# ScalarE's weight casts run one product further ahead of VectorE's low parts, and the first block's transfers go by quarters

## The chip, the core and the metric

The kernel runs on one core of a Trainium2 chip. The metric is device time in microseconds (us) of one execution. The core has five engines with an instruction queue each: TensorE (PE in the profile; its weight loads are PEld), VectorE (DVE), ScalarE (ACT), GpSimd (POOL) and SyncE (SP), which here only issues transfers. Each queue runs in its own order, and engines wait for each other through semaphores. An instruction whose wait is not over holds up all that stands behind it on its engine.

## The reference

One layer of an encoder, on 512 + 256 tokens of width 1024, in float32:

```python
x = layer_norm(ALPHA * x + 0.5 * swiglu(x, ffn1_up, ffn1_down), ln1_g, ln1_b)
u = x @ w_in
...
mix = (jax.nn.sigmoid(gate_a) * h_a + jax.nn.sigmoid(gate_b) * h_b) @ w_out
x = layer_norm(ALPHA * x + mix, ln2_g, ln2_b)
x = layer_norm(ALPHA * x + 0.5 * swiglu(x, ffn2_up, ffn2_down), ln3_g, ln3_b)

def swiglu(x, w_up, w_down):
    gate, up = jnp.split(x @ w_up, 2, axis=-1)
    return (jax.nn.silu(gate) * up) @ w_down
```

The change touches the two feed-forward blocks (`swiglu`, inner width 2816). Between them lie a recurrent branch, a retention branch and their merge, which the diff leaves alone.

## The kernel before, in words

**Numbers in two parts.** A float32 matrix is multiplied as two parts: a high part, which is the value rounded by a cast (`ph` for weights, `xh` or `eh` for inputs), and a low part, which is the value minus the high part (`pl`, `xl`, `el`). ScalarE makes the high part with one copy, VectorE the low part with one subtraction that reads the high part. So a low part always waits for ScalarE. A product is high by high, high by low and low by high: with four pieces of 128 rows it takes 12 matmuls into one bank (`mmt`, L210), eight with `ph` first and four with `pl` last.

**Seven products for eight.** The up projection treats, for each of the 22 column blocks `j`, the gate and the up weights and the two halves of the tokens and of the width as a 2 by 2 by 2 problem, and does it with seven products of 128 x 384 (`pair_items`, numbers 1 to 7). The products 1, 2, 3 and 4 of a `j` take weights as they come, or sums of them; 5, 7, 6 and 3 need sums of weight pieces, which VectorE makes (`combine`, tile `sa`, L376). On the other side, four kinds of input forms (T1, T3, T2, T4, in `forms`) are differences of token halves: for each, VectorE computes a difference (tile `f`, L295), ScalarE casts it (L320) and VectorE makes the low part (L314). They are made once a block, in its first steps, and every later product reads them.

**The order of the work.** `body` puts all products of a block, up and down, in one list of items, and walks over it with a step counter `t`. The queues of ScalarE, VectorE and TensorE are written out in exactly this order. A step does, in turn: the work on the result of product t-1 (`post`: ScalarE copies it to `u` at L414 or applies Silu at L420; VectorE adds at L409), then the transfers that are due (`ahead`, `AHEAD` items ahead), the weight sums that are due (`extra`), both parts of the weights of product t+2 (`prep`), up to three VectorE instructions of the forms (`advance`), and then the matmuls of product t. The first block begins its forms at t = 4 and the second at t = 6 (`FORMS`). The parts `ph` and `pl` have four buffers each, the raw weight pieces (`wr`, 128 x 512, 256 KB) have ten.

**The first items of a block.** For the first six `j` the list opens with twelve products that need no weight sum (`OPEN`: numbers 1 and 2 of each `j`), then 5, 7, 6 of the first two `j`, and then their 3 and 4. The 19th item of the list is product 3 of the first `j`. It adds onto the bank of product 5, which VectorE first has to read: that is the third of three adds after product 6 (L409). All this I call the opening of a block.

**Transfers.** SyncE issues all weight and input transfers in program order. At the very start (`first`, `inputs`) it issues weight pieces of the products 1 and 2 (`wr<-in_f1u`) and the token matrix (`z<-in_xT`, 16 transfers of 128 x 384, 192 KB: eight pieces of the width by two halves of the tokens). A transfer into a `wr` buffer waits until the low part or the sum that last read this buffer is done.

Of the kernel before, what the change touches and what calls it, by code (L numbers as in the profile page):

```python
# [8 lines left out]
F32 = mybir.dt.float32  # L9
F32R = mybir.dt.float32r  # L10
BF16 = mybir.dt.bfloat16
AF = mybir.ActivationFunctionType
ALU = mybir.AluOpType
# [5 lines left out]
P = 128  # L19
D = 1024  # L20
KT = D // P
# [33 lines left out]
TH = T // 2  # L55
LEAD = 6
OPEN = [(1, 0), (1, 1), (1, 2), (1, 3), (2, 0), (2, 1), (1, 4), (1, 5), (2, 2), (2, 3), (2, 4), (2, 5)]
FORMS = {True: 4, False: 6}
RAWS = 10
AHEAD = 9  # L60
GATED = 6
KEEPO = 4
TQ = 2
# [8 lines left out]
class Builder:  # L72
# [44 lines left out]
    def load(self, name, shape, pool=None):  # L117
        t = (pool or self.const).tile(shape, F32, name=self.nm(name))
        self.nc.sync.dma_start(t, self.I[name])
        return t  # L120
# [209 lines left out]
    def ffn(self, ctx, z, xs, idx, up, down, after, start, own, then=None):  # L330
        nc = self.nc
        chunks, j = [], 0
# [5 lines left out]
        m = KT // 2  # L338
        xe, fw = self.pool(ctx, "xe", 1), self.pool(ctx, "fw", 1)
# [25 lines left out]
                raws[j, part, h], = raw(up[j, :, part, h * m:h * m + m])  # L365
            return raws[j, part, h]

        def pieces(src):
            n = src.shape[-1]
            h, l = (fw.tile([P, m * P], F32R, tag=t, name=self.nm(t), bufs=4)[:, :n] for t in ("ph", "pl"))  # L370
            self.split(src, h, l)
            return tuple(t.rearrange("p (a b) -> p a b", b=P) for t in (h, l))

        def combine(a, b, op, out=None):
# [4 lines left out]
        def pair_items(j):  # L379
            early = j < LEAD  # L380
            st = {}

            def sum_of(n):
                def run():
                    g0, g1, u0, u1 = [load(j, p, h) for p in range(2) for h in range(2)]
                    if n == 1:
                        st[1] = combine(u0, u1, ALU.add)
                    elif n == 3:
                        st[3] = combine(g0, u0, ALU.subtract)
                    elif n == 2:  # L390
                        st[2] = combine(st[1], g0, ALU.subtract, st[1] if early else None)
                    else:
                        st[4] = combine(g1, st[2], ALU.subtract, st[2] if early else None)
                return run
# [5 lines left out]
            def bank_of(n):  # L400
                key = {1: "A", 2: "A", 5: "C", 3: "C", 7: "D", 4: "D", 6: "B"}[n]
                if key not in st:
# [3 lines left out]
            src = {1: lambda: load(j, 0, 0), 2: lambda: load(j, 0, 1), 4: lambda: load(j, 1, 1),  # L406
                   5: lambda: st[1], 7: lambda: st[3], 6: lambda: st[2], 3: lambda: st[4]}
# [32 lines left out]
            items = {}  # L440
            of = {5: 1, 7: 3, 6: 2, 3: 4}
            for n in (1, 5, 7, 6, 2, 3, 4):
                def mm(w, n=n):
                    alloc()
                    ps = bank_of(n)
                    self.mmt(ps, self.terms(w, X[xof[n]]), ((0, TH),), n not in (2, 3, 4), True, n in (2, 3, 4))
                    if early and n < 3:
                        raws.pop((j, 0, n - 1))
                need = (sum_of(of[n]), 3 if early else 6 + (n in (6, 3))) if n in of else None
                get = (lambda n=n: load(j, 0, n - 1)) if early and n < 3 else None  # L450
                items[n] = src[n], mm, *(lambda n=n, f=f: f(n) for f in (post, late, after_late)), need, get, xof[n]
            return items, lambda: [load(j, p, h) for p in range(2) for h in range(2)]
# [32 lines left out]
        def body():  # L485
# [16 lines left out]
            for i, it in enumerate(items):  # L502
                if it[6]:
                    fetch.setdefault(i, []).append(it[6])
                if it[5]:
                    extra.setdefault(max(i - it[5][1], -2), []).append(it[5][0])
            steps = self.forms(z, xs, ext, hp, own)

            def advance(t):
# [21 lines left out]
                        f()  # L531

            def prep(t):
                if t < len(items):
                    ready[t] = pieces(items[t][0]())

            ahead(0)
            with self.tc.manual_schedule(engines={E.Activation, E.DVE, E.PE}):
                for t in range(-2, len(items) + 1):
                    if t > 0:  # L540
                        items[t - 1][2]()
                    for f in afters:
                        f()
                    ahead(t)
                    if then and t == 100:
                        with self.tc.issue_after(self.mark):
                            then()
                    for f in extra.get(t, ()):
                        f()
                    prep(t + 2)  # L550
                    advance(t)
                    if t > 0:
                        items[t - 1][3]()
                        afters = [items[t - 1][4]]
                    if 0 <= t < len(items):
                        items[t][1](ready.pop(t))
                for f in afters:
                    f()
# [704 lines left out]
    def first(self, ctx):  # L1263
# [3 lines left out]
        xs = [self.xpair() for _ in range(KT)]  # L1267

        def inputs(load):
            for a in (0, TH):  # L1270
                for h in range(2):
                    load(0, 0, h)
                    for k in range(KT // 2 * h, KT // 2 * (h + 1)):
                        nc.sync.dma_start(z[k][:, a:a + TH], I["xT"][:, k, a:a + TH])
                    if a == 0:
                        for j in range(1, 4 - 2 * h):
                            load(j, 0, h)

        def after(seg, mean, lp):
            if seg[0] == 0:  # L1280
# [90 lines left out]
```

## Time and profile before

| what | value |
|---|---|
| time, median of 3 runs | 2006.35 us (2000.07, 2006.35, 2010.59) |
| the profiled execution, its own time | 1999.83 us |
| its span, first to last instruction | 1998.0 us |
| TensorE busy in the span | 1891.1 us (95%) |
| VectorE busy | 1261.1 us (63%) |
| ScalarE busy | 809.4 us (41%) |
| weights of the first block's products issued | 0.8 to 525.1 us |
| weights of the second block's products issued | 1426.0 to 1955.1 us |

In the views, an entry such as `L199 ACT CAST ph<-wr` is line 199 of the kernel, on ScalarE, that writes tile `ph` from tile `wr`. In brackets, or behind `<-`, stands for how long its engine had been idle before and what ended that. The busy time of TensorE is modelled, and overlaps from one matmul to the next; how many matmuls (`x...`) fall into a stretch tells more than its busy time.

### The profile page before, as it was taken

What the parts mean: (1) busy time and instruction counts of PE and PEld (TensorE: products, weight loads), DVE (VectorE), ACT (ScalarE), POOL (GpSimd) and SP (SyncE); (2) the same over time, 40 slices, a digit from 0 to 9 for tenths busy, and PEclk for the clock granted to TensorE, in tenths of its full rate; (3) what the DMA queues carried; (4) which work ended last, traced back from release to release, by engine and by line L of the source; (5) the groups of instructions that cost most, each with busy time, mean ns of one, the idle gap of its engine ahead of it and who ended that gap; (6) DMA issues with size and microseconds to landing.
All of it is one profiled execution on the core that took longest, in us unless ns stands there. A gap on an engine that the chain in (4) does not pass through costs nothing.

```text
span 1998.0 us, 33175 instructions
## 1 busy us (share of the span) xinstructions
PE 1891.1 (95%) x13098; PEld 1686.9 (84%) x13098; DVE 1261.1 (63%) x2208; ACT 809.4 (41%) x1521; POOL 190.4 (10%) x290
## 2 busy tenths in 40 slices
PE   7999999999989999999799989999879999999997
PEld 6899999999768778887688867789779999899985
DVE  5965746656755686768445555386679467375665
ACT  5332323323454353445244555332553234142325
POOL 0000000000000264445610000000000000000000
PEclk9999999999989999999999989999999999999998
DMA  6222222121332433333554442554222221212221
GB/s 195 85 74 75 66 72 75 53 85 45 108 103 84 146 120 127 113 129 120 154 162 132 127 121 73 202 166 139 69 85 90 75 74 56 83 56 72 66 72 65
DMA packets 141595, 200.48 MB, mean 100 GB/s; under 512 B 55680, under 2 KB 73728, under 8 KB 141440
## 3 DMA queue, kind: packets, MB, share of 16 engines
q1 hardware_dynamic: 123904, 176.35, 28.1%
q0 software_dynamic: 3424, 14.94, 2.2%
q10 hardware_dynamic: 14112, 7.08, 1.2%
q8 instruction: 103, 1.69, 0.4%
q14 instruction: 52, 0.43, 0.1%
HBM read 156.64 MB, written 41.68 MB: 99 GB/s over the span
## 4 chain that ended last, share of the span: by engine, by line
PE 79%; DVE 9%; DMA 4%; ACT 4%; issue 2%; SPq 0%; ACTq 0%; DVEq 0%; POOLq 0%
PE mm L210 39%; PE pc L210 28%; PE pc L255 2%; PE mm L644 2%; PE pc L109 2%; PE pc L1060 1%; DMA t<-gd 1%; PE w L996 1%; ACT ph L199 1%; DVE u L409 1%; PE pc L1108 1%; PE w L1007 1%; PE pc L701 1%; DVE f L295 1%; DVE z L283 1%
## 5 line engine op out<-in xcount | busy, mean ns | idle before, releaser
L210 PE MATMUL pc<-xh,ph 128*128 128x384 f32 x704 | 242.7, 345 | 22.4 <-DVE u L409 7.5
L210 PE MATMUL pc<-xl,ph 128*128 128x384 f32 x704 | 239.1, 340 | 3.1 <-DVE xl L314 3.0
L199 ACT CAST ph<-wr 128x512 fp32r<-128x512 f32 (+1 forms) x232 | 130.8, 567 | 217.9 <-PE mm L210 139.5
L210 PE MATMUL mm<-xh,wh 128*128 128x512 f32 (+1 forms) x640 | 177.5, 356 | 15.8 <-DVE osq L245 5.2
L210 PE MATMUL mm<-xl,wh 128*128 128x512 f32 (+1 forms) x640 | 170.4, 346 | 0.0
L200 DVE TENSOR_TENSOR pl<-wr,ph 128x512 fp32r<-128x512 f32 (+1 forms) x232 | 141.7, 622 | 44.6 <-ACT ph L199 43.5
L210 PE MATMUL pc<-eh,ph 128*128 128x384 f32 x480 | 161.1, 336 | 2.7 <-ACT ph L199 2.7
L409 DVE TENSOR_TENSOR u<-u,pc 128x384 f32<-128x384 f32 x208 | 114.9, 552 | 76.9 <-PE pc L210 73.8
L210 PEld LDWEIGHTS pc<-xh,ph 128*128 128x128 f32 x704 | 134.2, 191 | 31.5 <-issue 11.2
L210 PE MATMUL pc<-el,ph 128*128 128x384 f32 x480 | 160.5, 334 | 0.0
L210 PE MATMUL pc<-xh,pl 128*128 128x384 f32 x704 | 152.5, 338 | 0.0
L200 DVE TENSOR_TENSOR pl<-sa,ph 128x512 fp32r<-128x512 f32 x176 | 121.0, 687 | 43.6 <-ACT ph L199 43.5
L210 PE MATMUL mm<-hl,ph 128*128 128x512 f32 (+1 forms) x544 | 138.8, 336 | 0.0
L210 PE MATMUL mm<-hh,ph 128*128 128x512 f32 (+1 forms) x544 | 138.8, 336 | 0.0
L210 PEld LDWEIGHTS pc<-xl,ph 128*128 128x128 f32 x704 | 134.3, 191 | 4.5 <-DVE xl L314 4.4
L171 DVE TENSOR_TENSOR wl<-wr,wh 128x1024 fp32r<-128x1024 f32 (+1 forms) x68 | 74.6, 1098 | 96.8 <-PE mm L210 49.4
L210 PEld LDWEIGHTS mm<-xh,wh 128*128 128x128 f32 x640 | 102.0, 193 | 37.7 <-issue 15.6
L199 ACT CAST ph<-sa 128x512 fp32r<-128x512 f32 x176 | 106.3, 617 | 59.9 <-DVE sa L376 29.4
L210 PEld LDWEIGHTS pc<-xh,pl 128*128 128x128 f32 x704 | 126.4, 190 | 0.0
L210 PE MATMUL mm<-xh,wl 128*128 128x512 f32 (+1 forms) x640 | 125.1, 345 | 0.0
L170 ACT CAST wh<-wr 128x1024 fp32r<-128x1024 f32 (+1 forms) x68 | 62.7, 922 | 140.2 <-PE mm L210 112.7
L210 PEld LDWEIGHTS mm<-xl,wh 128*128 128x128 f32 x640 | 100.9, 193 | 16.8 <-issue 2.5
(319 smaller groups left out, 3965.9 us busy)
## 6 DMA issues: line engine op xcount, KB each, us to landing
wr<-in_f1u SPq DMA_DIRECT2D x100, 256.0 KB, 2.9
wr<-in_f2u SPq DMA_DIRECT2D x100, 256.0 KB, 2.9
wr<-in_w_in SPq DMA_DIRECT2D x30, 512.0 KB, 3.5
wr<-in_f1d SPq DMA_DIRECT2D x37, 256.0 KB, 2.7
wr<-in_f2d SPq DMA_DIRECT2D x37, 256.0 KB, 2.7
wr<-in_w_in SPq DMA_DIRECT2D x32, 256.0 KB, 3.6
dd<-ar SPq DMA_DIRECT2D x8, 768.0 KB, 3.3
dd<-kb SPq DMA_DIRECT2D x8, 768.0 KB, 4.5
```

The lines of the kernel that those rows point to most:

```text
L109: self.nc.tensor.matmul(ps, w, x[:, a:b], start=True, stop=True)
L170: nc.scalar.copy(hi, raw)
L171: nc.vector.tensor_tensor(out=lo, in0=raw, in1=hi.bitcast(F32), op=ALU.subtract)
L199: self.nc.scalar.copy(hi, src)
L200: self.nc.vector.tensor_tensor(out=lo, in0=src, in1=hi.bitcast(F32), op=ALU.subtract)
L210: self.latest = self.nc.tensor.matmul(o, w, x[:, a:b], start=start and i == 0, stop=stop and i == len(terms) - 1, skip_group_check=more).ins
L255: self.summed = nc.tensor.matmul(st["ps"], self.ones, src, start=k == 0, stop=k == KT - 1).ins
L283: nc.vector.scalar_tensor_tensor(out=zk, in0=zk, scalar=-0.5, in1=rs, op0=ALU.mult, op1=ALU.mult)
L295: tt = lambda o, a, b, op: lambda: nc.vector.tensor_tensor(out=o, in0=a, in1=b, op=op)
L409: add = lambda o, a, b: nc.vector.tensor_tensor(out=o, in0=a, in1=b, op=ALU.add)
L644: nc.tensor.matmul(dst, x[:, ts], w[:, :, k % 4], start=(k == 0 and q == 0), stop=(k == KT - 1 and q == 2))
L701: nc.tensor.matmul(op, v[:, a // P + j], x[:, j, :n], start=(j == 0 and q == 0), stop=(j == nj - 1 and q == 2))
```

## The change

Three things are edited.

`pieces` is divided into `high` (ScalarE's cast) and the rest (VectorE's subtraction). In step t, `prep` now issues the cast for product t+3 and the subtraction for product t+2, whose cast was issued a step before. The walk begins a step earlier (t = -3). For this the sums of weights of the early `j` are due four products ahead instead of three (product 3 of a `j` stays at three), transfers are issued ten items ahead instead of nine, and the first block begins its forms at t = 5 instead of 4.

The transfers at the start go by quarters of the token matrix: first half of the width and then the second, for the first half of the tokens; then the same for the second half of the tokens, with four more weight pieces ahead of its last quarter.

Nothing else is edited. No instruction is added or removed on any of the engines. Between the two blocks, where the scheduler places the instructions, a few of the group normalisation in the recurrent branch (L1119 to L1134 of the kernel before) move by up to eleven places; all others keep their order.

```diff
-FORMS = {True: 4, False: 6}
+FORMS = {True: 5, False: 6}
 RAWS = 10
-AHEAD = 9
+AHEAD = 10
...
-        def pieces(src):
-            n = src.shape[-1]
-            h, l = (fw.tile([P, m * P], F32R, tag=t, name=self.nm(t), bufs=4)[:, :n] for t in ("ph", "pl"))
-            self.split(src, h, l)
+        def high(src):
+            h = fw.tile([P, m * P], F32R, tag="ph", name=self.nm("ph"), bufs=4)[:, :src.shape[-1]]
+            nc.scalar.copy(h, src)
+            return src, h
+
+        def pieces(src, h=None):
+            if h is None:
+                src, h = high(src)
+            l = fw.tile([P, m * P], F32R, tag="pl", name=self.nm("pl"), bufs=4)[:, :src.shape[-1]]
+            nc.vector.tensor_tensor(out=l, in0=src, in1=h.bitcast(F32), op=ALU.subtract)
             return tuple(t.rearrange("p (a b) -> p a b", b=P) for t in (h, l))
...
-                need = (sum_of(of[n]), 3 if early else 6 + (n in (6, 3))) if n in of else None
+                need = (sum_of(of[n]), 4 - (n == 3) if early else 6 + (n in (6, 3))) if n in of else None
...
-                    extra.setdefault(max(i - it[5][1], -2), []).append(it[5][0])
+                    extra.setdefault(max(i - it[5][1], -3), []).append(it[5][0])
...
             def prep(t):
-                if t < len(items):
-                    ready[t] = pieces(items[t][0]())
+                if t + 1 < len(items):
+                    ready[t + 1] = high(items[t + 1][0]())
+                if 0 <= t < len(items):
+                    ready[t] = pieces(*ready[t])
...
-                for t in range(-2, len(items) + 1):
+                for t in range(-3, len(items) + 1):
...
         def inputs(load):
-            for a in (0, TH):
-                for h in range(2):
-                    load(0, 0, h)
-                    for k in range(KT // 2 * h, KT // 2 * (h + 1)):
-                        nc.sync.dma_start(z[k][:, a:a + TH], I["xT"][:, k, a:a + TH])
-                    if a == 0:
-                        for j in range(1, 4 - 2 * h):
-                            load(j, 0, h)
+            def quarter(a, h):
+                for k in range(KT // 2 * h, KT // 2 * (h + 1)):
+                    nc.sync.dma_start(z[k][:, a:a + TH], I["xT"][:, k, a:a + TH])
+
+            gates = lambda h, *js: [load(j, 0, h) for j in js]
+            gates(0, 0)
+            quarter(0, 0)
+            gates(0, 1, 2, 3)
+            quarter(0, 1)
+            gates(1, 0, 1)
+            quarter(TH, 0)
+            gates(0, 4, 5)
+            gates(1, 2, 3)
+            quarter(TH, 1)
```

**The order of SyncE's transfers at the start.** Rows are in the order of issue. `z_78` to `z_85` are the eight pieces of the width; the first eight transfers of `z` (the first half of the tokens) are out already. Before, from the sixth weight piece to the seventh:

```order
L352 DMA wr_137<-in_f1u 128x512
L1274 DMA z_78<-in_xT 128x384
L1274 DMA z_79<-in_xT 128x384
L1274 DMA z_80<-in_xT 128x384
L1274 DMA z_81<-in_xT 128x384
L1274 DMA z_82<-in_xT 128x384
L1274 DMA z_83<-in_xT 128x384
L1274 DMA z_84<-in_xT 128x384
L1274 DMA z_85<-in_xT 128x384
L352 DMA wr_151<-in_f1u 128x512
```

Now, from the sixth to the seventh:

```order
L352 DMA wr_137<-in_f1u 128x512
L1280 DMA z_78<-in_xT 128x384
L1280 DMA z_79<-in_xT 128x384
L1280 DMA z_80<-in_xT 128x384
L1280 DMA z_81<-in_xT 128x384
L352 DMA wr_143<-in_f1u 128x512
```

The seventh weight piece (the first of `j` = 4) stands four transfers of 192 KB further ahead.

**ScalarE in the opening of the first block.** The stretch is steps 9 and 10. The casts `ph` are for the 12th and 13th product before; the Silu (`u<-pc`) is that of the product just finished; the casts `eh` are forms. Before:

```order
L420 ACTIVATE u_232<-pc_234 128x384
L199 CAST ph_398<-wr_226 128x512
L320 CAST eh_111<-f_149 128x384
L420 ACTIVATE u_264<-pc_266 128x384
L199 CAST ph_423<-sa_396 128x512
```

Now, in the same two steps, where the casts are for the 13th and 14th product (L370 is the old L199, L426 the old L420):

```order
L426 ACTIVATE u_246<-pc_248 128x384
L370 CAST ph_402<-sa_375 128x512
L320 CAST eh_117<-f_158 128x384
L320 CAST eh_111<-f_157 128x384
L426 ACTIVATE u_266<-pc_268 128x384
L370 CAST ph_426<-sa_400 128x512
```

Behind the same Silu now stands the cast for one product later.

**VectorE in the same two steps.** `sa` are sums of weight pieces, `pl` the low parts, `f` and `el` the forms. Before:

```order
L376 TENSOR_TENSOR sa_396<-wr_250,wr_252 128x512
L200 TENSOR_TENSOR pl_399<-wr_226,ph_398 128x512
L314 TENSOR_TENSOR el_116<-f_150,eh_115 128x384
L295 TENSOR_TENSOR f_149<-f_149,z_78 128x384
L314 TENSOR_TENSOR el_118<-f_150,eh_117 128x384
L376 TENSOR_TENSOR sa_421<-wr_256,wr_258 128x512
L200 TENSOR_TENSOR pl_424<-sa_396,ph_423 128x512
```

Now (L382 is the old L376, L377 the old L200):

```order
L382 TENSOR_TENSOR sa_400<-wr_238,wr_240 128x512
L377 TENSOR_TENSOR pl_404<-wr_206,ph_377 128x512
L295 TENSOR_TENSOR f_158<-z_85,z_81 128x384
L314 TENSOR_TENSOR el_116<-f_158,eh_115 128x384
L295 TENSOR_TENSOR f_157<-f_157,z_78 128x384
L382 TENSOR_TENSOR sa_424<-wr_230,wr_232 128x512
L377 TENSOR_TENSOR pl_428<-sa_375,ph_402 128x512
```

The low part of the 12th product (`pl_399` before, `pl_404` now) stands in the same step, but the cast that it reads (`ph_377`) was issued a step earlier; in this step ScalarE casts `ph_402`, which VectorE reads a step later. The number of instructions from the seventh low part to the third add after product 6 is the same on VectorE in both.

## The prediction, made before the result was known

> **What bounds the kernel now.** I read the page first, then the busy times by stretch, then the waits in the stretches that are not full.
>
> ```profile
> PE   7999999999989999999799989999879999999997
> DVE  5965746656755686768445555386679467375665
> PE mm L210 39%; PE pc L210 28%; PE pc L255 2%; PE mm L644 2%; PE pc L109 2%; PE pc L1060 1%; DMA t<-gd 1%; PE w L996 1%; ACT ph L199 1%; DVE u L409 1%; PE pc L1108 1%; PE w L1007 1%; PE pc L701 1%; DVE f L295 1%; DVE z L283 1%
> ...
> 19.00:62.00 43.00, 31.93 (x162) 29.41 (x163) 32.32 (x61) 21.51 (x43) 0.00 (x0) 0.96 0.36 120
> 62.00:110.00 48.00, 48.00 (x268) 47.76 (x269) 44.39 (x73) 17.48 (x29) 0.00 (x0) 0.96 0.31 94
> 110.00:480.00 370.00, 369.37 (x2122) 350.82 (x2122) 226.34 (x369) 119.24 (x225) 0.00 (x0) 1.00 0.22 68
> 1454.00:1494.00 40.00, 30.62 (x163) 28.07 (x162) 30.91 (x57) 19.85 (x40) 0.00 (x0) 0.98 0.24 80
> 1494.00:1550.00 56.00, 55.37 (x312) 54.49 (x310) 51.21 (x84) 21.08 (x36) 0.00 (x0) 0.98 0.28 90
> 1550.00:1900.00 350.00, 350.00 (x2013) 332.21 (x2013) 209.88 (x332) 110.52 (x208) 0.00 (x0) 1.00 0.22 69
> ```
>
> The first two rows are the page's busy tenths, the third the lines of the chain that ended last. Below are stretches: start, end, length, then busy time and count of TensorE, its weight loads, VectorE, ScalarE and GpSimd, the clock, and transfers. TensorE sets the end: most of the chain is its matmuls (L210). In the body of both feed-forward blocks it has no gap (369.37 of 370 us, 350 of 350), so nothing gained on another engine there counts. A full stretch gives its pace: 370 / 2122 = 0.174 us a matmul, so a product of 12 takes 2.09 us.
>
> The openings are different. From 19 to 62 us only 162 matmuls run, work for 28.2 us at that pace; from 1454 to 1494 us 163, for 28.4 us. So 14.8 and 11.6 us are lost there. Who is waited for?
>
> ```profile
> ACT eh L320 <- DVE f L295: 14.3, 12, 2.1
> DVE pl L200 <- ACT ph L199: 12.4, 11, 2.9
> ...
> DVE pl L200 <- ACT ph L199: 8.0, 9, 1.6
> DVE pl L200 <- PE pc L210: 0.8, 1, 0.8
> ...
> 40.96 0.69 DVE L200 TENSOR_TENSOR pl<-sa,ph 128x512 fp32r<-128x512 f32 x1 [0.41 <-ACT ph L199]
> ...
> 42.51 0.55 DVE L295 TENSOR_TENSOR f<-f,z 128x384 f32<-128x384 f32 x1
> 42.98 0.68 DVE L376 TENSOR_TENSOR sa<-wr,wr 128x512 f32<-128x512 f32 x1
> 44.53 0.69 DVE L200 TENSOR_TENSOR pl<-sa,ph 128x512 fp32r<-128x512 f32 x1 [0.88 <-ACT ph L199]
> ...
> 43.09 0.51 ACT L320 CAST eh<-f 128x384 fp32r<-128x384 f32 x1 [0.42 <-DVE f L295]
> 43.51 0.48 ACT L420 ACTIVATE u<-pc 128x384 f32<-128x384 f32 x1
> 43.90 0.61 ACT L199 CAST ph<-sa 128x512 fp32r<-128x512 f32 x1
> ```
>
> The first two rows are waits of 19 to 62 us (total, times, longest), the next two all that VectorE waited for in 1454 to 1494 us; the rest is one turn of the loop. VectorE makes a form's difference (42.51), and only then can ScalarE cast it (43.09); behind that cast stand the Silu and the weight cast (43.90), and VectorE cannot make the low part before that cast (44.53). Each engine waits for the other once a product. VectorE waits for nothing but this cast, and TensorE follows:
>
> ```profile
> 21.18 0.50 PE L210 MATMUL pc<-xl,ph 128*128 128x384 f32 x1 [2.97 <-DVE xl L314]
> ...
> 37.88 0.45 PE L210 MATMUL pc<-xh,ph 128*128 128x384 f32 x1 [1.22 <-ACT ph L199]
> ...
> 61.85 0.41 PE L210 MATMUL pc<-xh,ph 128*128 128x384 f32 x1 [3.29 <-DVE u L409]
> ...
> 62.49 0.53 PE L210 MATMUL pc<-xl,ph 128*128 128x384 f32 x1
> 62.81 0.53 PE L210 MATMUL pc<-xh,ph 128*128 128x384 f32 x1
> ...
> 1493.09 0.66 PE L210 MATMUL pc<-xh,ph 128*128 128x384 f32 x1 [4.20 <-DVE u L409]
> ...
> 59.98 0.55 DVE L409 TENSOR_TENSOR u<-u,mm 128x384 f32<-128x384 f32 x1
> 60.56 1.14 DVE L409 TENSOR_TENSOR u<-u,pc 128x384 f32<-128x384 f32 x2
> ...
> 1491.81 1.14 DVE L409 TENSOR_TENSOR u<-u,pc 128x384 f32<-128x384 f32 x2
> ```
>
> The opening ends when the 19th product starts (61.85 and 1493.09), and it waits for VectorE's third add. So the end of an opening is VectorE's: its work in order plus its waits.
>
> **The casts one product ahead.** The low part of product t+2 now reads a cast issued a step before. ScalarE's step is a Silu or copy, a weight cast and one or two form casts; by the distances in the rows above (43.09, 43.51, 43.90) the first two cost 0.4 and, by a cast of 0.61, at most 0.6 us, so with two form casts a step is about 1.9 us. VectorE's step with a sum is 0.6 + 0.6 + 3 times 0.47 = 2.6 us. ScalarE therefore finishes its step inside VectorE's, and VectorE's waits for the cast should close. A form's low part could become the new wait, but another form instruction and mostly a sum stand between a difference and its low part, about as long as a cast.
>
> First block. The stretch that counts runs from the seventh low part to the third add:
>
> ```profile
> 18.85 0.62 ACT L199 CAST ph<-wr 128x512 fp32r<-128x512 f32 x1 [1.33 <-DMA wr<-in_f1u]
> ...
> 19.50 0.69 DVE L200 TENSOR_TENSOR pl<-wr,ph 128x512 fp32r<-128x512 f32 x1 [2.32 <-ACT ph L199]
> ...
> 20.58 0.55 DVE L314 TENSOR_TENSOR xl<-z,xh 128x384 fp32r<-128x384 f32 x1
> ```
>
> It takes 61.70 - 19.50 = 42.2 us. The 12.4 us of waits include the 2.32 before 19.50, so 10.1 lie inside and 32.1 are work. The instructions in it are the same before and now. If all waits close, 10.1 us are gained.
>
> **The quarters.** The seventh low part waited for its weight piece: the cast at 18.85 is the first that a transfer held up. In the new order four `z` transfers of 192 KB, 786 KB, no longer stand ahead of it.
>
> ```profile
> 0.00:19.00 19.00, 13.12 (x55) 11.36 (x55) 7.80 (x13) 10.38 (x20) 0.21 (x4) 1.00 0.88 282
> 20.00:30.00 10.00, 8.81 (x42) 8.81 (x43) 5.79 (x12) 5.51 (x10) 0.00 (x0) 0.83 0.80 277
> 9.89 4.44 SPq L1274 DMA_DIRECT2D z<-in_xT  x8
> 14.50 5.55 SPq L352 DMA_DIRECT2D wr<-in_f1u  x10
> ```
>
> At the 282 GB/s of the first 19 us that is 2.8 us; the eight `z` took 4.44 us to issue, so four are 2.2. I take 2.6: cast at 16.3, low part at 16.9. TensorE's stop of 2.97 us before 21.18 ends with `xl` (20.58), two instructions behind that low part, so it moves with it to about 18.6 and a stop of some 0.5 us is left. VectorE's third add then ends at 16.9 + 32.1 = 49.0 instead of 61.7: 12.7 us for the block. TensorE allows it: 162 matmuls from 18.6 at 0.174 us end at 46.8. The other side of this edit is that the second halves of `z` land later, behind weight pieces: the difference that first needs the last quarter stands a dozen instructions behind the seventh low part, some 6 us, and I count nothing; at worst it gives back the 2.6.
>
> Second block. Here no transfer order changes. VectorE's nine waits for the cast are 8.0 us, and the third add ends that much earlier, at 1484.9. TensorE allows that too: in its stretch it has 11.6 us to spare. I count 8.0 us; the extra cast now placed among the squares of the preceding layer norm costs 0.6 us of an engine that waits there, and I count nothing.
>
> **What stays at nothing.** The sums that are due a product earlier are the same instructions. Ten items ahead for transfers instead of nine gives the earlier casts their data; the cover is that TensorE never waits for a cast from 110 us on. After an opening TensorE is full, so what is gained is kept. The moved instructions in the recurrent branch are two normalisations of one ScalarE pass (0.84 us) each: 0, within 2 us either way.
>
> ```profile
> L1120 ACT ACTIVATE finz<-finy 128x768 f32<-128x768 f32 x2 | 1.7, 842 | 9.8 <-DVE finy L1119 9.8
> ```
>
> **TensorE's pace after a stop.** Behind the stop of 3.29 us the matmuls follow each other at 0.32 us (62.49, 62.81) instead of 0.174, behind that of 1.22 us they don't. About eleven slow ones cost 1.6 us. The new stops before the 19th product come out at 49.1 - 46.8 = 2.3 us in the first block, between these two rows, so the slow start may go or stay: 0 to 1.6 us in each block, kept for the range. [...]
>
> **The sum.** 10.1 + 2.6 + 8.0 = 20.7 us: the profiled execution's 1999.83 us (1998.0 of span and 1.8 around it) becomes 1979. The runs shown are 2000.07, 2006.35 and 2010.59, so their median lies 6.5 us above the profiled one; the same gain from the median is 1986. I take 1982, between the two.
>
> **The rivals.**
>
> *Half the waits come back.* ScalarE still waits for every difference (14.3 us in 12 waits), and its weight cast now stands between a difference and the form cast more often. If a form's low part waits 0.45 us in each of the 11 steps with forms, both openings lose 5 us again: gain 11, from the 2003 that the forecast starts from to 1992. For it: the ring between the engines is only cut at one place. Against: VectorE had no wait at all for a form cast in either opening.
>
> *The first block runs into its transfers.*
>
> ```profile
> wr<-in_f1u SPq DMA_DIRECT2D x100, 256.0 KB, 2.9
> ```
>
> The sums read pieces 14 to 18, and the ring of ten raw buffers lets a piece start only after a low part. 15 pieces and all `z` are 7.1 MB; at 282 GB/s until 19 us and 277 after they are in at 25.2 us, and by my count VectorE wants them at about 25. If it then waits at each of four sums for a transfer, 2.9 us from issue to landing by this row, the first block's gain shrinks by 11.6 to 1, the total to 9: 1994, no change that can be told. Against: pieces that wait are issued together, and their waits overlap.
>
> *Slower: the cast runs into the ring of raw buffers everywhere.* A cast is issued a product earlier, but the buffer that its piece needs is freed by a low part whose place has not moved.
>
> ```profile
> ACT ph L199 <- DMA wr<-in_f1d: 4.4, 2, 2.2
> ACT ph L199 <- DMA wr<-in_f1u: 4.4, 3, 1.5
> ```
>
> In 110 to 480 us ScalarE waits for a piece five times, so ten times in two blocks. Each wait would grow by a product, 2.1 us, or 4.2 for a down product of 24 matmuls, 3.1 in the middle: 31 us on ScalarE, and behind a waiting cast stand the copies and Silus that free TensorE's banks. It decides once a piece is later than the lead of three products, 6.3 us. Then 31 lost less 20.7 gained is 10 slower: 2013. Against: TensorE shows 0.6 us without matmuls in that whole stretch, and a wait of 2.2 us lies well inside 6.3.
>
> **How the numbers follow.** Forecast 0.70, half 0.12, transfers 0.10, slower 0.08. About 0.5%, 10 us, is what a measurement of this kernel can tell from no change. The forecast is faster throughout its own range, 1972 to 1990; the half case, with a gain of 11, is faster in somewhat over half its cases, and the transfers in a third. That makes faster 0.80, same 0.12, slower 0.08. The range reaches down for the slow start gone in both blocks and runs as fast as the profiled one (1999.83 - 24 = 1976, less 5 for spread), and up to the two middle cases with the same spread: 1971 to 1998.
>
> **What would show it.** VectorE's waits for the weight cast nearly gone in both openings; the 19th products at about 49 and 1485 - 12.7 = 1472 us; the seventh cast near 16.3; TensorE full behind them as before. It is wrong if the form casts or transfers take the waits' place there, or if TensorE shows waits for casts after 110 us.

## The result, and the profile after

| | before | after |
|---|---|---|
| median of 4 runs each | 2003.21 us (1998.45 to 2010.59) | 1970.99 us (1969.44 to 1974.73) |
| the profiled execution | 1999.83 us | 1969.44 us |
| its span | 1998.0 us | 1967.7 us |

The ratio is 0.984 [0.980, 0.988]: the change takes 32 us by the medians (25 to 40 by the interval) and 30.3 us between the two profiled spans. Forecast were 1982 us and a gain of 20.7 us. So the direction is right, the time lies 11 us under the forecast and at the lower end of the stated range (1971 to 1998 us, 0.01 us below it), and the gain is half as large again as the sum that I made.

First the page of the changed kernel, the busy tenths of TensorE and VectorE in 40 slices, then its busy times by stretch (the same columns as in the prediction):

```profile
PE   8999999999889999999799989999899999999997
DVE  8956737566737595868445555386789377375655
```

```profile
19.00:49.00 30.00, 28.12 (x163) 27.83 (x162) 29.52 (x59) 19.55 (x40) 0.00 (x0) 1.00 0.48 161
...
110.00:480.00 370.00, 370.00 (x2121) 351.11 (x2119) 217.40 (x361) 117.86 (x218) 0.00 (x0) 1.00 0.22 69
1434.00:1464.00 30.00, 26.47 (x152) 25.86 (x151) 28.20 (x55) 18.59 (x37) 0.00 (x0) 1.00 0.30 97
1464.00:1520.00 56.00, 56.00 (x314) 55.76 (x315) 51.98 (x85) 22.17 (x38) 0.00 (x0) 0.97 0.29 90
```

The first digit of VectorE went from 5 to 8, and its count in 19 to 49 us is 59 instructions in 29.52 of 30 us; before, 61 took 43. As many matmuls as needed 43 us before (162) now fit into 30 (163). In the second opening VectorE is busy 28.20 of 30 us. The waits in these two stretches:

```profile
ACT eh L320 <- DVE f L295: 5.7, 10, 1.6
DVE pl L377 <- ACT ph L370: 0.4, 1, 0.4
...
ACT eh L320 <- DVE f L295: 7.3, 12, 1.1
DVE pl L377 <- DMA wr<-in_f2u: 1.6, 1, 1.6
```

The first two rows are 19 to 49 us, the others 1434 to 1464 us. VectorE's waits for the weight cast went from 12.4 us in 11 to 0.4 us in one (the wait before the seventh low part, 2.32 us before and 1.61 now, lies inside the first stretch before and ahead of it now). In the second opening they went from 8.0 us in nine to the one wait of 1.6 us in the last row. The view puts that wait down to a transfer, but the timeline shows the cast again:

```profile
1433.62 1.28 ACT L426 ACT_TABLE_LOAD   x1
1434.92 0.49 ACT L426 ACTIVATE u<-pc 128x384 f32<-128x384 f32 x1
1435.30 0.61 ACT L370 CAST ph<-wr 128x512 fp32r<-128x512 f32 x1
...
1435.95 0.69 DVE L377 TENSOR_TENSOR pl<-wr,ph 128x512 fp32r<-128x512 f32 x1 [1.62 <-DMA wr<-in_f2u]
```

The low part starts 0.04 us after the end of the cast that it reads, and this cast stands behind a Silu whose table ScalarE loads for 1.28 us. The kernel before has the same wait of 1.62 us (at 1456.40), and there, as in the changed kernel's second profile, the view puts it down to the cast. ScalarE's waits for a difference are still there, but behind this one place VectorE no longer waits for ScalarE in turn. One piece of VectorE's queue in the second opening shows it:

```profile
1445.39 0.68 DVE L382 TENSOR_TENSOR sa<-wr,wr 128x512 f32<-128x512 f32 x1
1446.00 0.68 DVE L377 TENSOR_TENSOR pl<-sa,ph 128x512 fp32r<-128x512 f32 x1
1446.60 0.55 DVE L314 TENSOR_TENSOR el<-f,eh 128x384 fp32r<-128x384 f32 x1
1447.07 0.55 DVE L295 TENSOR_TENSOR f<-z,z 128x384 f32<-128x384 f32 x1
1447.54 0.55 DVE L314 TENSOR_TENSOR el<-f,eh 128x384 fp32r<-128x384 f32 x1
1448.00 0.68 DVE L382 TENSOR_TENSOR sa<-wr,wr 128x512 f32<-128x512 f32 x1
```

No row has a bracket, so the profile counts no idle time before any of them. Sum to sum takes 1448.00 - 1445.39 = 2.6 us; this is the VectorE step of the prediction. The points in time that the prediction named are these, in the trace of the changed kernel:

```profile
16.12 0.62 ACT L370 CAST ph<-wr 128x512 fp32r<-128x512 f32 x1 [0.87 <-DMA wr<-in_f1u]
...
16.78 0.69 DVE L377 TENSOR_TENSOR pl<-wr,ph 128x512 fp32r<-128x512 f32 x1 [1.61 <-ACT ph L370]
...
48.55 0.41 PE L210 MATMUL pc<-xh,ph 128*128 128x384 f32 x1 [1.88 <-DVE u L415]
48.80 0.34 PE L210 MATMUL pc<-xl,ph 128*128 128x384 f32 x1
48.98 0.33 PE L210 MATMUL pc<-xh,ph 128*128 128x384 f32 x1
...
1463.87 0.41 PE L210 MATMUL pc<-xh,ph 128*128 128x384 f32 x1 [3.17 <-DVE u L415]
```

The seventh cast runs at 16.12 (16.3 forecast), its low part at 16.78 (16.9), the first block's 19th product at 48.55 (49), and behind it the matmuls follow at full pace. TensorE still waits for the third add before both 19th products, 1.88 and 3.17 us.

So the openings did what was forecast. Where did the other ten microseconds come from? The next table follows both programs by the start of the nth TensorE matmul in each trace, and gives how much earlier the changed kernel gets there. All numbers are us.

| place | start before | ahead by |
|---|---|---|
| first matmul | 5.00 | 0.0 |
| 19th product, first block | 61.85 | 13.31 |
| two products later | 67.68 | 14.87 |
| the last wait for a cast behind the opening | 116.81 | 15.95 |
| 99 us before the first block's end | 459.24 | 15.97 |
| first block's end | 558.42 | 17.35 |
| last matmul before the second block's opening | 1425.49 | 20.70 |
| first product, second block | 1450.18 | 21.48 |
| 19th product, second block | 1493.09 | 29.23 |
| 56 us later | 1549.30 | 30.20 |
| last matmul | 1987.90 | 30.33 |

The two openings carry 13.3 and 7.7 us, 21.1 together. Behind the first come 1.6 us at once, 1.1 us until 117 us, 1.4 at the block's end, 3.4 us between the blocks, 0.8 just ahead of the second block, and 1.0 behind the second opening. One pair of traces can't tell which of these small terms repeat. The experiments had to.

### The profile page after: what moved, and what is told of

It is laid out like the page before. It is cut to its first block, busy times and chain, and to the rows that moved or that the text cites. A ratio compares the mean times of both kernels' runs of the same rounds, so it can differ in the third digit from the quotient of the medians.

```text
span 1967.7 us, 33187 instructions
## 1 busy us (share of the span) xinstructions
PE 1881.7 (96%) x13098; PEld 1684.1 (86%) x13098; DVE 1255.0 (64%) x2208; ACT 816.2 (41%) x1521; POOL 190.4 (10%) x290
## 4 chain that ended last, share of the span: by engine, by line
PE 82%; DVE 8%; DMA 4%; ACT 4%; issue 1%; SPq 0%; ACTq 0%; DVEq 0%; POOL 0%; POOLq 0%
PE mm L210 39%; PE pc L210 29%; PE pc L109 2%; PE mm L652 2%; PE pc L255 2%; PE pc L1068 1%; DMA t<-gd 1%; PE w L1004 1%; PE pc L1116 1%; PE pc L709 1%; PE w L1015 1%; PE mm L829 1%; DVE z L283 1%; PE pc L1077 1%; PE w L1009 1%
## 5 line engine op out<-in xcount | busy, mean ns | idle before, releaser
L370 ACT CAST ph<-wr 128x512 fp32r<-128x512 f32 (+1 forms) x232 | 131.4, 569 | 276.7 <-PE mm L210 143.7
L377 DVE TENSOR_TENSOR pl<-wr,ph 128x512 fp32r<-128x512 f32 (+1 forms) x232 | 140.5, 620 | 11.2 <-ACT ph L370 9.4
L370 ACT CAST ph<-sa 128x512 fp32r<-128x512 f32 x176 | 105.7, 616 | 77.2 <-DVE sa L382 33.0
L377 DVE TENSOR_TENSOR pl<-sa,ph 128x512 fp32r<-128x512 f32 x176 | 119.5, 684 | 0.7 <-ACT ph L370 0.7
```

The source lines that it names most:

```text
L370: nc.scalar.copy(h, src)
L377: nc.vector.tensor_tensor(out=l, in0=src, in1=h.bitcast(F32), op=ALU.subtract)
```

## The experiments

My theory: the gain is VectorE's freed waits in the two openings, the casts carry nearly all of it, the quarters some 2 us, and what is over the 20.7 us are small stops behind the openings that the same edit removes. The rivals: the quarters carry a large part of the first block; or the surplus comes from the moved instructions between the blocks, or from the tenth transfer ahead; or it is only the scatter between executions.

Four kernels with one part each ran in one session, beside 16 runs of the kernel before (median 2001.19 us).

### The quarters alone

The kernel before, with only `inputs` exchanged:

```diff
-            for a in (0, TH):
-                for h in range(2):
...
+            gates(0, 0)
+            quarter(0, 0)
+            gates(0, 1, 2, 3)
...
```

> The kernel before with the new order of transfers at the start and nothing else. Theory (the quarters act alone, by the transfer that the seventh low part waits for): the seventh low part comes 2.5 us sooner, the 19th product starts at 59 instead of 61.9 us, total gain 2 to 3 us, ratio 0.9987. Rival (they pay only with VectorE freed of the casts): the stop before 21 us shrinks, but the 19th product starts at 61 to 62 us, no gain in total.

Measured: 1999.33 us (10 runs), ratio 0.9992 [0.9977, 1.0008]. VectorE's waits from 14 to 62 us (13.6 us in 14 in the kernel before), TensorE's wait for `xl` (3.0 us before), and ScalarE up to the seventh cast:

```profile
DVE pl L200 <- ACT ph L199: 13.4, 13, 2.9
...
PE pc L210 <- DVE xl L314: 1.5, 1, 1.5
...
17.75 0.48 ACT L414 COPY u<-pc 128x384 f32<-128x384 f32 x1 [1.08 <-PE pc L210]
18.12 0.62 ACT L199 CAST ph<-wr 128x512 fp32r<-128x512 f32 x1
```

The 19th product starts at 61.14, against 61.85, 61.82 and 61.49 in three profiles of the kernel before: 0.6 us earlier than their mean. The theory wanted 59, the rival 61 to 62 with a shorter stop before 21 us: the rival came true. By itself the new order of transfers gives no gain that can be told. The seventh cast no longer waits for its piece, but it stands behind a copy, and this copy waits 1.08 us for TensorE's product. So the cast comes at 18.12, which is 0.7 us earlier than before and not 2.5, and from its low part (18.78) to the third add (60.99) VectorE takes 42.2 us as before.

### The casts alone

The changed kernel with the old `inputs`.

> The changed kernel with the old order of transfers. Theory: VectorE's waits for casts close as in the changed kernel; the 19th product starts 2.5 us later than there, at 51 us; gain 27 to 28 us, ratio 0.986. Rival (most of what the first block gained came with the transfers): the 19th product starts after 55 us, gain below 24.

Measured: 1976.66 us (4 runs), ratio 0.987 [0.984, 0.990]. VectorE's waits for the cast from 14 to 62 us, then TensorE's from 10 to 125:

```profile
DVE pl L377 <- ACT ph L370: 5.2, 5, 3.3
...
PE pc L210 <- DVE xl L314: 2.2, 1, 2.2
PE pc L210 <- DVE u L415: 1.6, 1, 1.6
```

and the seventh cast in the timeline:

```profile
18.29 0.62 ACT L370 CAST ph<-wr 128x512 fp32r<-128x512 f32 x1 [2.62 <-DMA wr<-in_f1u]
```

The 19th product starts at 51.96, 9.8 us earlier than the mean of the kernel before (10.1 forecast for this part). Three profiles of the changed kernel have it at 48.55, 49.37 and 50.35, so the quarters add 1.6 to 3.4 us once VectorE has no other wait (2.6 forecast). VectorE's wait of 3.3 us is for the seventh cast, whose piece is late: it runs at 18.29, in the changed kernel at 16.12. TensorE's stop of 2.2 us before a form's `xl` follows from it, and in the changed kernel that stop is 0.4 us. The two parts of the change are not independent: the transfers' order gives 0.6 us alone, where the seventh cast waits for TensorE's product, and 2.5 in the mean on top of the casts, where it stands a product earlier.

### One block at a time

In each of these the lead of the casts, of the sums and of the transfers, the first step and the beginning of the forms are those of the changed kernel in one block alone (`A` is 1 there and 0 in the other); the one for the second block has the old `inputs`. The diff leaves out some lines.

```diff
+        A = int(own)          # second block alone: int(not own)
-                need = (sum_of(of[n]), 4 - (n == 3) if early else ...
+                need = (sum_of(of[n]), 3 + A * (n != 3) if early else ...
-                while done < min(t + AHEAD, len(items) - 1):
+                while done < min(t + AHEAD - 1 + A, len(items) - 1):
-                if t + 1 < len(items):
-                    ready[t + 1] = high(items[t + 1][0]())
+                if t + A < len(items):
+                    ready[t + A] = high(items[t + A][0]())
-                for t in range(-3, len(items) + 1):
+                for t in range(-2 - A, len(items) + 1):
```

> The change in the first block alone; the second is as before. Between the blocks the scheduler's order is that of the changed kernel. Theory (the change acts where it is, and the order between the blocks is worth 2 us): the first block ends 18 us sooner, between the blocks 2 us are gained, the second gains nothing; gain 20, ratio 0.990. Rival (what was gained between the blocks is scatter): gain 16 to 22 with between the blocks anything from -2 to +3 us.

> The change in the second block alone. Between the blocks the order is exactly that of the kernel before. Theory: first block unchanged to 0.3 us, between the blocks unchanged to 0.5 us, the second gains 10 us; ratio 0.995. Rival (scatter between the blocks): between the blocks differs from the kernel before by 1 to 3 us although the order is the same.

Measured: the first block alone 1984.34 us (4 runs), 0.992 [0.989, 0.995], 16.9 us less than before; the second alone 1989.16 us (7 runs), 0.994 [0.992, 0.996], 12.0 us less. The theories were 20 and 10 us. Together 28.9 us: the blocks add up to about the whole, and each gives more than its opening. By the starts of the matmuls the opening of the first block is 11.6 us shorter and that of the second 7.6. TensorE's waits from 10 to 125 us, of the one with the first block, then of the one with the second:

```profile
PE pc L210 <- DVE u L416: 2.4, 1, 2.4
```

```profile
PE pc L210 <- ACT ph L371: 4.6, 6, 1.2
PE pc L210 <- DVE u L416: 3.3, 1, 3.3
PE pc L210 <- DVE xl L314: 2.5, 1, 2.5
PE mm L210 <- ACT ph L371: 1.7, 2, 0.9
```

With the casts ahead the eight waits for the cast (first and last row) are gone, those behind the opening among them.

### The kernels profiled again, and nine ahead

To tell small terms from scatter, the kernel before and the changed kernel were profiled again in a second session, with one variant: the changed kernel with `AHEAD = 9`.

> The kernel before, unchanged, for a second profile. Theory (the stretch between the blocks scatters from execution to execution): from the end of the first block to the first product of the second it takes 1.5 us or more longer or shorter than in the first profile, while both openings repeat to 0.5 us. Rival (the changed kernel's order gains there): it repeats to 0.5 us.

> The changed kernel, unchanged, for a second profile and more times. Theory: both openings repeat to 1.5 us (the first transfers and the slow matmuls behind the stop vary), between the blocks it gains anything from -1 to +4 us against the kernel before; median 1971 to 1975, ratio 0.984 to 0.987. Rival: it repeats the 3.4 us gained between the blocks to 0.5 us.

> The changed kernel with transfers nine items ahead instead of ten. Theory (casts never wait long for pieces, the ring of raw buffers sets when a transfer starts): openings and bodies as in the changed kernel to 0.5 us, no wait of TensorE for a cast. Rival (the tenth item is what feeds the earlier casts): ScalarE's waits for pieces grow by 2 us each and TensorE shows waits for casts after 110 us, 5 us or more in a block.

Measured: before 2003.54 us (one run; 2003.07 is the median of the session's seven others), the changed kernel 1972.87 us (4 runs), ratio 0.985 [0.983, 0.987], nine ahead 1976.27 us (one run). ScalarE's waits for weight pieces from 110 to 480 us, nine ahead (`in_f1u` are pieces of the up projection, `in_f1d` of the down projection):

```profile
ACT ph L370 <- DMA wr<-in_f1d: 7.5, 5, 1.5
ACT ph L370 <- DMA wr<-in_f1u: 7.4, 5, 1.5
```

and its busy times there:

```profile
110.00:480.00 370.00, 370.00 (x2121) 351.27 (x2121) 219.07 (x362) 118.73 (x219) 0.00 (x0) 1.00 0.22 69
```

With ten ahead, the changed kernel has in the same stretch:

```profile
ACT ph L370 <- DMA wr<-in_f1d: 11.2, 7, 2.2
ACT ph L370 <- DMA wr<-in_f1u: 8.9, 6, 1.5
```

ScalarE's waits for pieces did grow from the 4.4 and 4.4 us of the kernel before, and the tenth item ahead doesn't lower them. But TensorE is full with nine and with ten, and the second opening takes 35.20 us with nine and 35.17 with ten. The edit of `AHEAD` does nothing that the traces show; the 3.4 us between the times of the two kernels are within what one execution of either differs from the next.

A third session took one profile each of the same kernels and of the two with one block.

> The kernel before, a third profile, for the time from the end of the first block (the matmul before its layer norm's last sums) to the second block. In the profiles so far this stretch was, against the first profile of the kernel before: in its order of instructions 0, 3.2 and 1.4 us longer, and equal; in the order of the changed kernel 3.4, 3.2, 0.6 and 0.7 us shorter. Theory (scatter of 3 us whatever the order): anywhere from 4 longer to 3 shorter. Rival (the changed order is worth 3 us): 0 to 3 us longer.

> The changed kernel, a third profile. Theory (scatter): the stretch between the blocks anywhere from 4 us longer to 4 shorter. Rival (order): 0.5 to 3.5 us shorter. First opening: the 19th product starts 11.5 to 13.5 us sooner than before; slow matmuls behind it if its stop is 2.3 us or longer, none if it is 1.9 or shorter. Second opening 7.7 us, and 1.0 us behind it.

> The change in the first block alone, again; between the blocks it has the order of the changed kernel. Theory (scatter): the stretch between the blocks anywhere from 4 us longer to 4 shorter. Rival (order): 0.5 to 3.5 us shorter. Second opening as before.

> The change in the second block alone, again; between the blocks it has the order of the kernel before. Theory (scatter): the stretch between the blocks anywhere from 4 us longer to 3 shorter. Rival (order): 0 to 3 us longer. Second opening 7.7 us and 1.0 us behind it.

Measured, one run each: before 2004.18 us, the changed kernel 1979.49, the first block alone 1982.62, the second alone 1987.83. The third profile of the changed kernel is 10 us longer than its first; 6.7 us of that lie between the blocks. Its 19th product comes 11.4 us before the mean of the kernel before (11.5 to 13.5 expected), and its stop there, 2.38 us, is followed by slow matmuls, as expected. With three traces of each kernel the terms can be read with their spread. The rows are stretches between matmuls with the same number, in us:

| stretch | before, three profiles | changed, three profiles | difference of the means |
|---|---|---|---|
| to the 19th product, first block | 61.85, 61.82, 61.49 | 48.55, 49.37, 50.35 | 12.3 |
| slow matmuls behind its stop, over the full pace | 1.6, 1.6, 0.1 | 0.1, 1.5, 1.6 | 0.0 |
| the 50 us behind it | 49.13, 49.15, 49.11 | 48.04, 48.01, 48.01 | 1.1 |
| the first block's last 99 us | 99.19, 99.23, 98.60 | 97.80, 99.56, 98.10 | 0.5 |
| between the blocks | 867.07, 870.26, 873.58 | 863.72, 863.90, 870.41 | 4.3 |
| first to 19th product, second block | 42.91, 42.82, 42.77 | 35.17, 35.23, 35.19 | 7.6 |
| the 56 us behind it | 56.21, 56.48, 56.42 | 55.24, 55.21, 55.23 | 1.1 |
| the second block's last 72 us | 72.05, 73.12, 73.40 | 72.18, 72.18, 72.18 | 0.7 |

They sum to 27.6 us, against 28.2 between the means of the spans (1998.0, 2001.7, 2002.2 and 1967.7, 1971.7, 1977.7).

Two rows were not in my sum and repeat without overlap: the 50 and the 56 us behind the openings, 1.1 us each. They are the same in every kernel so far: 48.01 to 48.04 in all seven with the casts ahead in the first block, 49.11 to 49.15 in the six without, and 55.21 to 55.25 in six of the seven with the casts ahead in the second block (55.28 in the other), 56.21 or more without. What it is, the kernel before shows in TensorE's waits from 62 to 130 us (from 1497 to 1560 us the view gives the same row):

```profile
PE pc L210 <- ACT ph L199: 0.6, 2, 0.5
```

In the timeline:

```profile
111.89 0.44 PE L210 MATMUL pc<-eh,ph 128*128 128x384 f32 x1 [0.18 <-ACT ph L199]
...
116.81 0.44 PE L210 MATMUL pc<-xh,ph 128*128 128x384 f32 x1 [0.46 <-ACT ph L199]
```

Twice a block, shortly behind the opening, TensorE waited for a weight cast. The idle time is 0.64 us; counted by the starts of the matmuls, the two places cost 1.1 us. The changed kernel has no wait at all in these stretches.

The row between the blocks is not settled. Over all profiles with the order of the kernel before it is 867.07, 870.26, 873.58, 868.42, 867.03 and 867.35, and over those with the changed order 863.72, 863.90, 870.41, 863.31, 866.47, 864.56 and 866.43. The means are 869.0 and 865.5, but the two sets overlap, and one kernel alone spreads over 6.7 us. In the first pair of profiles and in each later session the mean is shorter with the changed order, by 2.8 to 5.1 us, on one or two profiles a side; the later sessions ran on three different chips. Of shorter pieces in between, one around 1175 to 1195 us is 2.1 us shorter with the changed order in the mean and shorter in every profile (17.12 to 18.64 against 19.15 to 20.57), but what lies ahead of it takes some of that back: from 1139 to 1199 us, around most of the places where the order differs, the mean is 0.6 us shorter and the sets overlap. Other pieces hold waits for transfers that vary. Around 1118 to 1139 us VectorE waited 2.1 us for one (`finz<-dd`) in the first profile of the kernel before and 3.8 in the second, and the piece took 20.1 and 23.5 us. Whether the changed order is worth 0 or 4 us, these runs don't tell; none of them has the changed order and nothing else.

### The bank of product 5 copied by ScalarE

Both 19th products of the changed kernel still wait for three adds in a row on VectorE, which stand behind product 6. ScalarE can empty the bank: it copies the result of product 5 a step earlier, so that the bank is free before the adds. VectorE still makes three adds, but none of them reads that bank.

```diff
+                elif n == 5:
+                    nc.scalar.copy(u[:, TH:], st["C"])
                 elif n == 6:
+                    add(u[:, TH:], u[:, TH:], st["D"])
                     add(u[:, :TH], u[:, :TH], st["B"])
-                    add(u[:, TH:], u[:, :TH], st["D"])
-                    add(u[:, TH:], u[:, TH:], st["C"])
+                    add(u[:, TH:], u[:, TH:], u[:, :TH])
```

> The changed kernel, where ScalarE copies the result of product 5 out of its bank as soon as it is made, so that the 19th product no longer waits for VectorE's third add. Theory (the stops before the 19th products, 1.9 and 3.2 us, come from this bank alone, and VectorE keeps up behind it): both stops go, no slow matmuls follow, gain 2 to 5 us on the changed kernel, ratio to the kernel before 0.982 to 0.984. Rival (VectorE's work sets the end of the opening whatever the bank does): the stops move to the next products and the gain is below 1 us.

Measured: 1962.21 us (1960.29 to 1969.61, 4 runs), ratio to the kernel before 0.979 [0.977, 0.981], and 10.7 us under the changed kernel in the same session. The last matmuls before the 19th product, and its start:

```profile
46.80 0.85 PE L210 MATMUL mm<-eh,pl 128*128 128x384 f32 x4
47.49 0.33 PE L210 MATMUL pc<-xh,ph 128*128 128x384 f32 x1
```

All waits of TensorE from 10 to 125 us:

```profile
PE pc L210 <- DVE pl L377: 0.9, 3, 0.4
```

The 19th product follows the one before without a gap, and so it does in the second block, whose opening goes from 35.2 to 31.2 us. That much was expected; the gain was more than twice the expected one. The rest lies at the ends of the blocks: the last 99 us of the first take 94.85 us (98.5 in the mean of the changed kernel's three profiles), the last 72 of the second 68.61 (72.18). The copy is made for every `j`, and two waits of TensorE near the end of the first block's up projection, 1.7 us for ScalarE's `hh` and 0.3 for VectorE's `hl` in the changed kernel (440 to 545 us), are gone. What the rest of these gains comes from stays open. Against this, TensorE now waits behind the openings for VectorE's low part: the 50 us behind the first become 49.89. Its profiled execution is the slowest of its four runs, with 874.09 us between the blocks, where it has an order of instructions of its own, so its span of 1967.8 us shows none of the gain. One piece there takes 25.1 us, against 18.9 to 20.1 in every other profile, and in it ScalarE waits 6.25 us for a transfer. By the times the version beats both kernels.

## Why the prediction was right, and where it failed

**The casts, 10.1 and 8.0 us: right.** Measured 9.8 us with the casts alone in the first block and 7.6 in the second, which came out alike within 0.15 us in every session. VectorE's waits for the cast closed as its step of 2.6 us said they would, but for one: the 1.6 us behind ScalarE's table load stayed in the second block, where the sum counted them as gained. The 0.8 us for which VectorE had waited for TensorE, and which the sum left out, went instead, so that the 7.6 near the forecast 8.0 are in part luck. That the waits of an engine that sets the end can be summed from one view, and taken for the gain, held here because its instructions stayed the same.

**The quarters, 2.6 us: right in size, but not by themselves.** On top of the casts they gave 1.6 to 3.4 us, and the seventh cast came at 16.12, 16.57 and 17.18 in the three profiles for 16.3. Alone they gave 0.6 us and no gain in time that can be told, because the cast then stands behind a copy that waits 1.08 us for TensorE's product. I had added the two terms as if each stood alone. The cast at 18.85 is also not "the first that a transfer held up": those at 3.92 and 9.23 us waited for transfers too, which changes nothing in the sum.

**"After an opening TensorE is full, so what is gained is kept": this step failed.** I counted nothing behind the openings, though two rows that I quoted showed something: 369.37 of 370.00 and 55.37 of 56.00 us busy, 0.63 us missing in each. I read 0.6 us as full, and said that "TensorE never waits for a cast from 110 us on". It did, at 111.89 and 116.81 us and again twice in the second block, and for just the instruction that the change moves ahead. By the matmuls that is 1.1 us a block, 2.2 us in all. In the changed kernel the same rows read 370.00 and 56.00. The ends of the blocks, which the sum left out, give 0.5 and 0.7 us in the mean, with spreads of that size.

**The moved instructions between the blocks, "0, within 2 us either way": open.** The means of all profiles differ by 3.5 us with overlapping sets, one piece is 2.1 us shorter in every profile and its neighbours take most of it back. If any large term was missed, it is here. So of the 28 us between the mean spans 20 are the openings as forecast, 2.2 are the stops behind them, 1.2 the block ends, and some 4 us lie in a stretch where two executions of one kernel differ by more.

**The slow restart, 0 to 1.6 us in each block: right as a range.** In the first pair of traces it went in the first block, which is 1.6 of its 30.3 us; in the three pairs it changed nothing. In the second block it stayed, in every profile with a stop. Before the first block's 19th product, stops of 2.28 and 2.38 us, near the 2.3 that the prediction had worked out, were followed by slow matmuls each time (below).

**The starting point.** The forecast starts from 2002.7 us (1982 + 20.7), and the medians of the kernel before are 2003.21, 2001.19 and 2003.07. The step to "between the two" was sound; the 11 us are all missing gain. Of these, 3.4 us are accounted for above (the stops and the block ends); the rest is the open stretch between the blocks and the scatter between executions. The range's lower end had 3.2 us for the slow starts, which did not go, and nothing for these terms.

**The rivals.** *Half the waits come back* fell: VectorE waits for no form's cast in either opening. *The first block runs into its transfers* fell: from 19 to 49 us VectorE waits for no transfer. *The ring of raw buffers everywhere* has its mechanism in the trace, not its price: ScalarE's waits for pieces went from 8.8 us in 5 to 20.1 in 13 between 110 and 480 us, none longer than 2.2 us, and the lead of three products that the prediction put at 6.3 us hid all of it: TensorE had no wait there.

## What to carry to other kernels

Here two engines that work in order waited for each other once a step, and issuing one of them a step ahead was worth about the sum of the other's waits: 9.8 us for 10.1, and 7.6 for 8.0. That sum can be read from the waits of the stretch where the waiting engine sets the end; leave out a wait with another cause, such as the one behind a table load. The same edit also removed the lone short waits of the same kind outside that stretch: before calling a stretch full, look up who ends its last few tenths, because the difference between 369.4 and 370 us can be the very wait that is being removed. And the earlier transfer was worth 0.6 us while the cast that reads it stood behind another wait, of 1.08 us, and 2.5 us once that wait was out of its way, so its price belongs in the sum only together with the edit that removes this wait.

## What the hardware showed that was not expected

**Slow matmuls behind a stop depend on more than its length.** Before the first block's 19th product TensorE stopped for 1.58, 1.88 and 1.90 us in three profiles, and its pace was full behind it each time. Stops of 2.28, 2.38 and 2.38 us were followed by slow matmuls each time, and of seven stops of 3.27 to 3.38 us five were. In the second block all thirteen stops of 3.14 to 4.23 us were. One of 2.28 us, in the second profile of the changed kernel:

```profile
49.37 0.66 PE L210 MATMUL pc<-xh,ph 128*128 128x384 f32 x1 [2.28 <-DVE u L415]
49.82 0.52 PE L210 MATMUL pc<-xl,ph 128*128 128x384 f32 x1
50.14 0.52 PE L210 MATMUL pc<-xh,ph 128*128 128x384 f32 x1
```

One of 3.27 us, in the third profile of the kernel before:

```profile
61.49 0.41 PE L210 MATMUL pc<-xh,ph 128*128 128x384 f32 x1 [3.27 <-DVE u L409]
61.74 0.34 PE L210 MATMUL pc<-xl,ph 128*128 128x384 f32 x1
61.92 0.35 PE L210 MATMUL pc<-xh,ph 128*128 128x384 f32 x1
```

And in the changed kernel's second block, behind the stop of 3.17 us, the pace is full at first and falls 0.9 us later:

```profile
1464.12 0.34 PE L210 MATMUL pc<-xl,ph 128*128 128x384 f32 x1
1464.29 0.34 PE L210 MATMUL pc<-xh,ph 128*128 128x384 f32 x1
...
1465.03 0.53 PE L210 MATMUL pc<-xh,ph 128*128 128x384 f32 x1
1465.35 0.53 PE L210 MATMUL pc<-xl,ph 128*128 128x384 f32 x1
```

Starts 0.17 us apart are the full pace, 0.32 the slow one; a slow stretch cost 1.4 to 2.8 us. Why stops of equal length end differently, and why the pace can fall late, these runs do not show. A stop of 2.28 us was enough, and one of 3.27 us was not.

**Equal programs spread where they wait for transfers.** The 870 us between the blocks, with such waits in them, differ by 6.7 us between profiles of the changed kernel, and the start of its first 19th product, behind the first transfers, by 1.8 us, while the second opening and the 50 us behind the first repeat to 0.15 us. The profiles are of different sessions and chips; that the transfers make the whole spread is not shown. A small term there can't be read from one pair of traces.
